# Applying a token norm on the outputs of the projections instead of on their input, and reordering gate products, FFN pairs and attention gates

## The chip, the cores and the metric

The kernel runs on one core of one Trainium2 chip, in one launch. The metric is the device time of that core in microseconds. "PE" is the matrix engine (TensorE), "PEld" its weight loads, DVE the vector engine, ACT the scalar engine, POOL the GpSimd engine and SP the engine that issues the large transfers.

## The reference

Two transformer blocks run one after the other on 256 tokens of width 2048, in fp32. The first has a neighbourhood attention of 16 heads and a convolutional FFN of width 5504. The change touches the FFN's first weights and the whole of the second block, whose core is:

```
def hybrid_layer(x, ...):
    h = rms_norm_2(x, norm_g)
    proj = jnp.einsum('bsd,dn->bsn', h, w_in)
    (q_a, k_a, v_a, o_a, i_a, f_a, z_a, c_q, c_kv, k_r, z_b, g_a, g_b) = jnp.split(proj, offsets, axis=-1)
    qk_a = jax.nn.silu(causal_depthwise_conv(jnp.concatenate([q_a, k_a], axis=-1), conv_w))
    ...
    h_a = mlstm_chunkwise(q_a, k_a, v_a, i_a + bias, f_a + bias)
    h_a = rms_norm_2(h_a, mlstm_norm_g)
    y_a = jnp.einsum('bsc,cd->bsd', jax.nn.sigmoid(o_a) * h_a * jax.nn.silu(z_a), w_a)
    q_b = jnp.einsum('bsr,rn->bsn', rms_norm_2(c_q, q_lat_g), w_uq)
    kv_b = jnp.einsum('bsr,rn->bsn', rms_norm_2(c_kv, kv_lat_g), w_ukv)
    ...
    o_b = causal_attention(q_b, k_b, v_b)
    y_b = jnp.einsum('bsc,cd->bsd', o_b * jax.nn.silu(z_b), w_b)
    y = jax.nn.sigmoid(g_a) * y_a + jax.nn.sigmoid(g_b) * y_b
    return x + jnp.einsum('bsd,de->bse', y, w_out)
```

`rms_norm_2(x, g)` is x times g times one factor per token, r = 1/sqrt(mean of x squared over the 2048 channels + 1e-6). Since r belongs to the token and the product with w_in runs over the channels, (x g r) w_in and ((x g) w_in) r are the same number. The mLSTM has 8 heads (q and k of 128, v of 256), the attention 16 heads (q and k of 128 + 64 with rotation by cos and sin of position times frequency, v of 128).

## The kernel before

*Products.* Everything is kept with channels on the 128 partitions and the 256 tokens along the free axis. An fp32 product is made of three reduced ones: a weight is split into a high half `whi` (a CAST on ACT) and a low half `wlo` (a subtraction on DVE), and so are the activations (`h` = [hH | hL], `hf`, `ya`, `ob`, `latkv`, ...). `GemmW` (L476) makes the products of one output chunk: per input chunk of 128 channels one matmul with `whi` over 512 columns (high and low half of the activation at once) and one with `wlo` over 256 columns. The two column halves of the PSUM bank are added when the bank is read (`fold`, L1056: a COPY on ACT, a sum on DVE).

*Units.* The program is a list of units. A unit is a weight load of 1 MB into one of three raw buffers and the matmuls that use it (`Unit`, L179), and it is split in two halves, each a tile of `whi` and one of `wlo` of 128x1024, from rings of 5. `pair_units` (L1070) cuts a product with 2048 input channels for `nj` output chunks (2 or 4; a bank per output chunk) into pairs of chunks, and each pair into two units: input chunks 0 to 7, then 8 to 15, with 32 matmuls each.

*Order.* The order of the instructions on every engine is fixed when the program is built. `run_units` (L389) goes through the units, and for each emits its matmuls; between them it polls a heap of pending steps (`spawn`, `poll`), which are Python generators: each emits a few instructions on DVE, ACT or POOL and says after which estimated delay it goes on (`yield 1.0`; a bare `yield` is "when the estimate of the last instruction ends"). `Engine` (L136) holds the estimates of cost, and `need` (L230) runs the heap until a condition holds, for instance that a ring has a free tile. The weight halves are emitted up to four ahead (`prep_ahead`, L373). So ACT's, DVE's and POOL's queues each hold weight work and bank work in one order, and an instruction that waits holds up all that stand behind it.

*The stages around the change, with their start in the trace.* In the FFN (`ffn_units`, L1239; from 750 us) a pair of gate chunks is followed by the pair of up chunks; its input chunks `hf` are made by DVE, 16 of them, and a matmul's `need` asks for the chunk it reads. The second block begins with `c_begin` (L1308; near 1490 us). Its input is `h2` = x times norm_g_2, split in halves. The sum of squares and r come from `stats_end` (L1041) as a row form `r2` (128x256, the same row on each partition). The first group of q, k and o products (g = 0 in `ml_qk`, `ml_o`) reads the `h2` that is not normalised, and multiplies its banks with `r2`. Meanwhile a loop in `c_begin` with `h2_again` (L1363) normalises `h2` in place, chunk by chunk: a sum on DVE (`mct`), a product with `r2` on POOL, a CAST on ACT (`hH`), a subtraction on DVE (`hL`). `counted` tells the loop how far the o products, which were put in turn with the k products for it, have read. All later products (`ml_v`, `misc`, `ml_z`, `latent`, `mla_z`, the gates) wait by `h2need` for the new chunks.

`rope_tables` (L1370) is spawned after that loop: two small loads on POOL's queue, an angle, its halves (`angh` by ACT), then some 50 small POOL steps that reduce it, then two ACT steps `rsin`, `rcos`, emitted after `yield 1.0`.

The eight mLSTM heads (`ml_head`, L1578) follow in pairs of heads, `W` being the masked and weighted score, `mv` the value, `ha` the head's output, which is transposed by PE (L265) and becomes `ya`. Then come `gated` units (L1940), four steps `cg` of: a gate product (4 output chunks of g_a), and the product `ya` times w_a for the same chunks, multiplied with the sigmoid (`sga`) when read. Then `latent` (L1663; `latq`, `latkv`, with a norm of their own through `cc`), the attention's heads in pairs: `mla_units` (L1836) are the q and kv products of a pair, `mla_z` (L1730) the four gates `zb` of two pairs, `mla_attn` (L1868) the head, with `bp` the scores after the exponential, `bpt` their transposes, `bv` the values and `ob` the gated output. Then four `gated` steps with g_b and w_b, and the last product.

Of the kernel before, what the change touches and what calls it, by code (L numbers as in the profile page):

```python
# [527 lines left out]
class Model(Kern):  # L528
# [512 lines left out]
    def stats_end(self, width, b, r):  # L1041
# [4 lines left out]
        yield from self.rsqrt(c[:, 0:2], c[:, 12:14], width, c[:, 4:8])  # L1046
        yield
        b = self.bank()
        self.spread(b.t, c[:, 0:2])
# [189 lines left out]
    def ffn_units(self):  # L1239
# [68 lines left out]
    def c_begin(self):  # L1308
# [3 lines left out]
        p = self.L.push("ya")  # L1312
        self.ya = p.tile([128, KD, 512], F32R, name="ya")
# [6 lines left out]
        self.sgring = Ring(self, p, "sga", [128, 256], F32, 5)  # L1320
# [7 lines left out]
        self.soring = Ring(self, p, "so", [128, 256], F32, 5)  # L1328
# [4 lines left out]
        self.fring = Ring(self, p, "fold2", [128, 256], F32, 3)  # L1333
# [12 lines left out]
        r = self.r2 = p.tile([128, 256], F32, name="r2")  # L1346
        self.c_ready = True
        yield from self.stats_end(D, sums, r)
        self.r_ready = True
        for m in range(KD):  # L1350
            while m >= self.early_done:
                yield 0.3
            yield from self.calm()
            t, i = self.cring.get()
            h, l = self.h2H[:, m], self.h2L[:, m]
            self.tt(t, h.bitcast(F32), l.bitcast(F32), ALU.add)
            yield
            self.tt(t, t, r, ALU.mult, e=self.G)
            self.spawn(self.h2_again(m, t, i), max(0.0, self.ct - self.now) + 0.1)
            yield  # L1360
        self.spawn(self.rope_tables(p), 1.0)

    def h2_again(self, m, t, i):  # L1363
        self.A.copy(out=self.h2H[:, m], in_=t)
        yield
        self.V.tensor_sub(out=self.h2L[:, m], in0=t, in1=self.h2H[:, m])
        self.cring.put(i)
        self.h2_ready.add(m)

    def rope_tables(self, p):  # L1370
# [34 lines left out]
        yield 1.0  # L1405
# [22 lines left out]
    def misc(self, out, b):  # L1428
        g8 = slice(0, 8)
        self.A.copy(out=self.krx2[0:64], in_=out[0:64])  # L1430
        a, z, ga, gb, gc = self.gi, self.gz, self.ga, self.gb, self.gc
        self.V.tensor_copy(out=a, in_=out[64:72])
        self.V.tensor_copy(out=z, in_=out[96:104])
# [65 lines left out]
    def h2need(self, k):  # L1499
        self.need(lambda: k in self.h2_ready)  # L1500
# [7 lines left out]
    def ml_qk(self, g, isq):  # L1508
        def evac(j, halves, b):
            h = 2 * g + j  # L1510
            blk = h if isq else 8 + h
            self.need(lambda: self.c_ready and (g or self.r_ready))
# [651 lines left out]
```

## Time and profile before

| | |
|---|---|
| median of 3 runs | 2649.54 us (2644.38 to 2654.28) |
| profiled execution | 2648.81 us |
| its span | 2647.0 us, mean granted clock 0.989 |
| HBM | 511.35 MB read, 196 GB/s over the span |
| DVE, low halves of weights | 822 instructions, 982.5 us, mean 1208 ns |
| ACT, high halves of weights | 822 instructions, 829.6 us, mean 1021 ns |
| chain that ended last | PE 91%, DVE 5%, ACT 2%, POOL 1% |

The profiled execution is one execution of the program; the span runs from its first to its last instruction. In a row of the timeline the numbers are start and busy time in us, then engine, line, operation, output<-inputs, shape and count, and in brackets the idle time ahead of it with what ended it. L151 is the line of the helper that emits every DVE, ACT and POOL instruction, so these are told apart by their tiles. In a window's row there are, per engine, busy us and (instructions), then PE's granted clock as a share of full speed, the busy share of the DMA engines and GB/s.

### The profile page before, as it was taken

Reading aid. Unit: us, or ns where it says so; the run is one execution under the profiler, and the core shown is the slowest. Engines: PE = TensorE matmul, PEld = TensorE weight load, DVE = VectorE, ACT = ScalarE, POOL = GpSimd, SP = SyncE. Lnnn points to the kernel's source line nnn. Section 1 sums busy time; section 2 is a strip of 40 time slices with the busy share of each in tenths; the row PEclk is TensorE's granted clock in tenths of the full one; section 3 lists DMA queues with packets and bytes.
Section 4 is the critical chain, followed back from the end, with each engine's and each line's share of the span. In section 5 each row is a group of like instructions: output and inputs, shape, how many; then the busy total and the mean of one; then the engine's idle time right before and its main releaser. Section 6 shows DMA issues by size and latency. Waiting matters only on the chain.

```text
span 2647.0 us, 40673 instructions
## 1 busy us (share of the span) xinstructions
PE 2563.6 (97%) x16038; PEld 2276.6 (86%) x16038; DVE 1824.0 (69%) x2962; ACT 1430.5 (54%) x2638; POOL 256.7 (10%) x279
## 2 busy tenths in 40 slices
PE   4999999999989999999999998999989999999999
PEld 2799999999968888888888877888878888888888
DVE  7987777677678887877555786567555566766654
ACT  5664444445555555555444556666644467775442
POOL 5421111111110000000000052000000000000000
PEclk8999999999999999999999999999999999999999
DMA  7886776665545666665565544554455533435554
GB/s 268 294 251 227 195 234 211 202 194 194 201 182 211 235 223 223 229 219 207 201 210 195 203 144 152 182 184 163 165 181 207 199 138 129 153 139 199 194 200 155
DMA packets 82543, 522.37 MB, mean 197 GB/s; under 512 B 9232, under 2 KB 15376, under 8 KB 23856
## 3 DMA queue, kind: packets, MB, share of 16 engines
q1 hardware_dynamic: 76656, 501.88, 53.2%
q0 software_dynamic: 5696, 17.90, 4.1%
q8 instruction: 126, 2.06, 0.3%
q14 instruction: 65, 0.53, 0.1%
HBM read 511.35 MB, written 8.39 MB: 196 GB/s over the span
## 4 chain that ended last, share of the span: by engine, by line
PE 91%; DVE 5%; ACT 2%; POOL 1%; issue 1%; DMA 0%; SPq 0%; DVEq 0%; ACTq 0%; POOLq 0%
PE bank L256 89%; DVE wlo L151 2%; PE bank L265 2%; POOL ry L151 1%; ACT whi L151 0%; ACT L149 0%; DVE hL L151 0%; DMA nx<-in_ctxT_dram 0%; DVE mct L151 0%; DVE h L151 0%; POOL racc L151 0%; DVE hf L151 0%; SPq L707 0%; POOL rn L151 0%; DVE cc L151 0%
## 5 line engine op out<-in xcount | busy, mean ns | idle before, releaser
L151 DVE TENSOR_TENSOR wlo<-raw,whi 128x1024 fp32r<-128x1024 f32 (+3 forms) x822 | 982.5, 1208 | 255.8 <-ACT whi L151 252.3
L151 ACT CAST whi<-raw 128x1024 fp32r<-128x1024 f32 (+3 forms) x822 | 829.6, 1021 | 414.0 <-PE bank L256 332.3
L256 PE MATMUL bank<-h,whi 128*128 128x512 f32 (+1 forms) x1696 | 597.5, 397 | 3.5 <-ACT whi L151 3.5
L256 PE MATMUL bank<-hf,whi 128*128 128x512 f32 x1376 | 484.9, 398 | 5.1 <-DVE hf L151 5.1
L256 PE MATMUL bank<-h,wlo 128*128 128x256 f32 x1680 | 473.0, 282 | 0.5 <-DVE wlo L151 0.5
L256 PEld LDWEIGHTS bank<-h,whi 128*128 128x128 f32 x1696 | 319.0, 189 | 78.0 <-ACT whi L151 3.7
L256 PE MATMUL bank<-hf,wlo 128*128 128x256 f32 x1376 | 385.8, 280 | 0.0
L256 PE MATMUL bank<-whi,hH 128*128 128x256 f32 x1280 | 366.6, 286 | 0.0
L256 PE MATMUL bank<-whi,hL 128*128 128x256 f32 x1280 | 362.4, 283 | 2.2 <-DVE hL L151 2.2
L256 PE MATMUL bank<-wlo,hH 128*128 128x256 f32 x1280 | 362.6, 283 | 1.2 <-DVE wlo L151 1.2
L256 PEld LDWEIGHTS bank<-h,wlo 128*128 128x128 f32 x1680 | 319.4, 190 | 1.1 <-DVE wlo L151 1.0
L256 PEld LDWEIGHTS bank<-hf,whi 128*128 128x128 f32 x1376 | 259.0, 188 | 68.8 <-DVE hf L151 7.3
L256 PEld LDWEIGHTS bank<-hf,wlo 128*128 128x128 f32 x1376 | 260.6, 189 | 0.0
L256 PEld LDWEIGHTS bank<-wlo,hH 128*128 128x128 f32 x1280 | 245.3, 192 | 2.4 <-DVE wlo L151 1.8
L256 PEld LDWEIGHTS bank<-whi,hL 128*128 128x128 f32 x1280 | 245.2, 192 | 2.5 <-DVE hL L151 2.4
L256 PEld LDWEIGHTS bank<-whi,hH 128*128 128x128 f32 x1280 | 245.2, 192 | 0.9
L256 PE MATMUL bank<-hid,whi 128*128 128x512 f32 x688 | 243.1, 399 | 0.0
L256 PE MATMUL bank<-hid,wlo 128*128 128x256 f32 x688 | 193.3, 281 | 0.0
L151 DVE SCALAR_TENSOR_TENSOR acc<-raw,cs,acc 128x512 f32<-128x512 f32 x240 | 186.8, 778 | 6.8
L256 PEld LDWEIGHTS bank<-hid,whi 128*128 128x128 f32 x688 | 129.3, 188 | 32.1
L151 ACT COPY fold<-bank 128x256 f32<-128x256 f32 x118 | 43.8, 372 | 165.4 <-PE bank L256 162.6
L256 PEld LDWEIGHTS bank<-hid,wlo 128*128 128x128 f32 x688 | 130.1, 189 | 0.0
(329 smaller groups left out, 3718.2 us busy)
## 6 DMA issues: line engine op xcount, KB each, us to landing
raw<-in_w_in_dram SPq DMA_DIRECT2D x120, 1024.0 KB, 4.9
raw<-in_w_ada_dram SPq DMA_DIRECT2D x86, 1024.0 KB, 4.9
raw<-in_ffn_w_up_dram SPq DMA_DIRECT2D x86, 1024.0 KB, 4.9
raw<-in_na_w_qkv_dram SPq DMA_DIRECT2D x42, 1024.0 KB, 4.9
raw<-in_ffn_w_down_dram SPq DMA_DIRECT2D x40, 1024.0 KB, 4.8
raw<-in_na_w_o_dram SPq DMA_DIRECT2D x16, 1024.0 KB, 5.3
raw<-in_w_a_dram SPq DMA_DIRECT2D x16, 1024.0 KB, 4.9
raw<-in_w_b_dram SPq DMA_DIRECT2D x16, 1024.0 KB, 4.9
```

Of the source, the lines that this page charges most:

```text
L151: r = f(*a, **kw)
L256: self.T.matmul(out, lhsT, rhs, start=start, stop=stop)
L265: self.T.transpose(out, in_, self.con("id"))
```

## The change

1. The loop in `c_begin`, `h2_again` and `counted` go. `h2` stays as it is, and each product that reads it multiplies its banks with `r2`, by one DVE instruction behind the `fold`: q, k, o of all groups, `ml_z`, `misc` (three small ones), `latent`, `mla_z`, the gates. `ml_v`, whose tokens are on the partitions, uses a column form `r2c` as the scale of its ACT step and the scalar of its DVE step; `stats_end` keeps that column. `r2` moves to a pool that lives to the end.
2. `gated` returns its gate units and its w units apart, and `ahead` orders them gate 0, gate 1, w 0, gate 2, w 1, gate 3, w 2, w 3. The ring of gate tiles grows from 5 to 8 and lives in another pool.
3. The first pair of the FFN is emitted as gate unit 0, up unit 0, gate unit 1, up unit 1.
4. `rope_tables` is spawned right after `r2`, and its sines wait 12.0 in place of 1.0 of estimated time.
5. The attention's z pairs stand one pair ahead: pair 0, then for each g pair g + 1 and the units of head pair g.
6. Rings: `fold2` from 3 to 2, `so` from 5 to 4; `latent` takes its scratch tile from another ring.

```
@@ stats_end @@
-    def stats_end(self, width, b, r):
+    def stats_end(self, width, b, r, rc=None):
...
-        yield from self.rsqrt(c[:, 0:2], c[:, 12:14], width, c[:, 4:8])
+        rc = c[:, 0:2] if rc is None else rc
+        yield from self.rsqrt(rc, c[:, 12:14], width, c[:, 4:8])
...
@@ ffn_units @@
+                if not c:
+                    first = [first[0], b[0], first[1], b[1]] if not gate else b
+                    if gate:
+                        continue
+                    b = first
@@ c_begin @@
+        self.sgring = Ring(self, p, "sga", [128, 256], F32, 8)
...
-        self.soring = Ring(self, p, "so", [128, 256], F32, 5)
+        self.soring = Ring(self, p, "so", [128, 256], F32, 4)
...
-        self.fring = Ring(self, p, "fold2", [128, 256], F32, 3)
+        self.fring = Ring(self, p, "fold2", [128, 256], F32, 2)
...
-        yield from self.stats_end(D, sums, r)
+        yield from self.stats_end(D, sums, r, self.r2c)
         self.r_ready = True
-        for m in range(KD):
-            while m >= self.early_done:
-                yield 0.3
-            yield from self.calm()
-            t, i = self.cring.get()
-            h, l = self.h2H[:, m], self.h2L[:, m]
-            self.tt(t, h.bitcast(F32), l.bitcast(F32), ALU.add)
-            yield
-            self.tt(t, t, r, ALU.mult, e=self.G)
-            self.spawn(self.h2_again(m, t, i), max(0.0, self.ct - self.now) + 0.1)
-            yield
         self.spawn(self.rope_tables(p), 1.0)
-    def h2_again(self, m, t, i):
-        self.A.copy(out=self.h2H[:, m], in_=t)
-        yield
-        self.V.tensor_sub(out=self.h2L[:, m], in0=t, in1=self.h2H[:, m])
-        self.cring.put(i)
-        self.h2_ready.add(m)
@@ rope_tables @@
-        yield 1.0
+        yield 12.0
         for t in (sin, cos):
             self.act(t, t, AF.Sin)
@@ h2need @@
-        self.need(lambda: k in self.h2_ready)
+        self.need(lambda: k in self.x2_ready)
@@ ml_qk @@
-            if g == 0:
-                self.tt(u, u, self.r2, ALU.mult)
-                yield
+            self.tt(u, u, self.r2, ALU.mult)
+            yield
@@ ml_v @@
-                    self.split(v[:, 0, j, 0:256], v[:, 1, j, 0:256], out[:, i * 256:i * 256 + 256])
+                    o, r = out[:, i * 256:i * 256 + 256], self.r2c[:, j:j + 1]
+                    self.act(v[:, 0, j, 0:256], o, AF.Copy, scale=r)
+                    self.stt(v[:, 1, j, 0:256], o, r, v[:, 0, j, 0:256].bitcast(F32), ALU.mult, ALU.subtract)
@@ ml_z, latent, mla_z, gated's evac_g, each behind its fold @@
+            self.tt(t, t, self.r2, ALU.mult)
+            yield
@@ gated @@
-        us = self.pair_units("w_in_2", KD, g0 + cg * 512, self.h2p, evac_g, nj=4)
+        gate = self.pair_units("w_in_2", KD, g0 + cg * 512, self.h2p, evac_g, nj=4)
...
-        return us + self.pair_units(w, KD, cg * 512, xs, evac_w, need, lambda: begin(cg), nj=4)
+        return gate, self.pair_units(w, KD, cg * 512, xs, evac_w, need, lambda: begin(cg), nj=4)
+
+    def ahead(self, jobs):
+
+        us = jobs[0][0][:]
+        for cg in range(4):
+            us += (jobs[cg + 1][0] if cg < 3 else []) + jobs[cg][1]
+        return us
@@ c_units @@
-                o = [o[0], o[2], o[1], o[3]]
-                for i in range(2):
-                    o[2 * i + 1].body = self.counted(o[2 * i + 1].body, i)
...
-        for g in range(4):
-            z = self.mla_z(g)
-            us += z[:2] + self.mla_units(2 * g) + z[2:] + self.mla_units(2 * g + 1)
+        z = [u for g in range(4) for u in self.mla_z(g)]
+        us += z[:2]
+        for g in range(8):
+            us += z[2 * g + 2:2 * g + 4] + self.mla_units(g)
```

How the built order moves is shown at three places. A number behind a name is that of a buffer.

ACT's queue where the sines stand. Before, behind the z gates (`mct`) of the first group of heads:

```order
L151 CAST whi<-raw 128x1024
L151 COPY mct_14991<-bank_15785 128x256
L151 CAST whi<-raw 128x1024 x2
L151 COPY mct_14992<-bank_15786 128x256
L151 ACTIVATE mct_14991<-mct_14991 128x256
L151 ACTIVATE rsin<-rsin 128x64
L151 ACTIVATE rcos<-rcos 128x64
L149 ACT_TABLE_LOAD
L151 ACTIVATE E_14998<-E_14998,acol 128x256
```

ACT's queue now: the high part of the angle, `angh`, right behind the first q copy (`mq`), and the sines behind the o gates (`so`), one weight half ahead of the first v copy (`mv`):

```order
L149 ACT_TABLE_LOAD
L151 ACTIVATE mct_14995<-mct_14995 128x256
L151 CAST mq_14983<-mct_14995 128x256
L151 CAST angh<-ang 128x64
L151 CAST whi<-raw 128x1024
L151 COPY fold_15007<-bank_15063 128x256
```

```order
L151 ACTIVATE so_15000<-so_15000 128x256
L151 ACTIVATE so_15001<-so_15001 128x256
L151 CAST whi<-raw 128x1024 x5
L149 ACT_TABLE_LOAD
L151 ACTIVATE rsin<-rsin 128x64
L151 ACTIVATE rcos<-rcos 128x64
L151 CAST whi<-raw 128x1024
L151 ACTIVATE mv_14989<-bank_15425,r2c 128x256
```

Between these two pieces lie 22 rows. The sines have moved from the z product of the first group to a place behind its o product, and `angh` from behind the first `mv` to ahead of it.

PE's queue at the last pair of mLSTM heads, where `W` meets `mv`, where `ha` is transposed and where the first w_a product reads `ya`. Before:

```order
L256 MATMUL bank_18597<-h_12991,whi 128x512
L256 MATMUL bank_18597<-h_12991,wlo 128x256
L256 MATMUL bank_18698<-mv_14985,W_14999 128x258 x3
L256 MATMUL bank_18702<-mv_14985,W_14999 128x258 x6
L265 MATMUL bank_18725<-cons,ha_15000 128x128 x2
L265 MATMUL bank_18725<-cons,ha_15001 128x128 x2
L265 MATMUL bank_18759<-cons,ha_15000 128x128 x2
L265 MATMUL bank_18759<-cons,ha_15001 128x128 x2
L256 MATMUL bank_18772<-ya,whi 128x512
L256 MATMUL bank_18772<-ya,wlo 128x256
```

Now the same two `W` rows, and the transposes of `ha` further down (the first `ya` row comes 32 rows behind them):

```order
L256 MATMUL bank_18680<-h_12991,whi 128x512
L256 MATMUL bank_18680<-h_12991,wlo 128x256
L256 MATMUL bank_18694<-mv_14990,W_15003 128x258 x3
L256 MATMUL bank_18698<-mv_14990,W_15003 128x258 x6
L256 MATMUL bank_18681<-h_12991,whi 128x512
L256 MATMUL bank_18681<-h_12991,wlo 128x256
```

```order
L256 MATMUL bank_18814<-h_12991,whi 128x512
L256 MATMUL bank_18814<-h_12991,wlo 128x256
L265 MATMUL bank_18867<-cons,ha_15004 128x128 x2
L265 MATMUL bank_18867<-cons,ha_15005 128x128 x2
L256 MATMUL bank_18813<-h_12991,whi 128x512
L256 MATMUL bank_18813<-h_12991,wlo 128x256
```

Between W and the transposes there are now rows of a gate product (`h`), where nothing stood before, and more of it between the transposes and `ya`.

PE's queue at the first attention heads, where keys (`bkt`) and scores (`bp`) are transposed. Before, a product of the next pair follows:

```order
L265 MATMUL bank_21074<-cons,bkt_20096 128x128 x2
L265 MATMUL bank_21075<-cons,bkt_20096 128x128
L265 MATMUL bank_21074<-cons,bkt_20096 128x128 x2
L265 MATMUL bank_21075<-cons,bkt_20096 128x128
L265 MATMUL bank_21082<-cons,bp_20100 128x128 x3
L265 MATMUL bank_21088<-cons,bp_20101 128x128 x3
L256 MATMUL bank_21104<-whi,latkv 128x512
L256 MATMUL bank_21104<-wlo,latkv 128x512
L256 MATMUL bank_21104<-whi,latkv 128x512 x2
```

Now the transposed scores of two heads (`bpt`) are used right behind:

```order
L265 MATMUL bank_21178<-cons,bkt_20097 128x128 x2
L265 MATMUL bank_21179<-cons,bkt_20097 128x128
L265 MATMUL bank_21178<-cons,bkt_20097 128x128 x2
L265 MATMUL bank_21179<-cons,bkt_20097 128x128
L265 MATMUL bank_21186<-cons,bp_20101 128x128 x3
L265 MATMUL bank_21193<-cons,bp_20102 128x128 x3
L256 MATMUL bank_21218<-bpt_20103,bv_20087 128x256 x3
L256 MATMUL bank_21218<-bpt_20103,bv_20087 128x128 x3
L265 MATMUL bank_21225<-cons,bsq_20096 128x128 x2
L265 MATMUL bank_21226<-cons,bx_20100 128x128
L265 MATMUL bank_21225<-cons,bsq_20096 128x128 x2
L265 MATMUL bank_21226<-cons,bx_20100 128x128
```

The first two heads of the attention are no longer separated from their own transposes by the next pair's `latkv` product.

## Rows read from the trace of the kernel before

**Rows 1.** The page, part 1: busy us (share of the span) x instructions
```profile
PE 2563.6 (97%) x16038; PEld 2276.6 (86%) x16038; DVE 1824.0 (69%) x2962; ACT 1430.5 (54%) x2638; POOL 256.7 (10%) x279
```

**Rows 2.** Windows of 50 us: PE, PEld, DVE, ACT, POOL, clock, DMA share, GB/s
```profile
1500.00:1550.00 50.00, 45.86 (x232) 38.61 (x231) 42.85 (x69) 31.38 (x52) 12.31 (x11) 0.93 0.49 169
1550.00:1600.00 50.00, 49.12 (x276) 41.59 (x276) 37.90 (x64) 24.53 (x43) 37.45 (x52) 1.00 0.46 153
1600.00:1650.00 50.00, 43.08 (x216) 35.73 (x215) 33.60 (x73) 36.15 (x64) 5.43 (x15) 0.93 0.36 125
1700.00:1750.00 50.00, 50.00 (x265) 42.48 (x264) 35.61 (x69) 39.91 (x70) 0.00 (x0) 1.00 0.43 148
1900.00:1950.00 50.00, 41.98 (x240) 36.64 (x239) 26.45 (x50) 29.86 (x51) 0.00 (x0) 0.93 0.43 148
1950.00:2000.00 50.00, 50.00 (x291) 44.11 (x290) 28.67 (x34) 24.09 (x33) 1.15 (x2) 1.00 0.57 197
2100.00:2150.00 50.00, 45.98 (x251) 39.24 (x251) 29.27 (x54) 27.45 (x48) 0.00 (x0) 0.97 0.42 143
2350.00:2400.00 50.00, 46.30 (x263) 40.06 (x262) 34.78 (x90) 34.66 (x84) 0.87 (x2) 0.93 0.36 127
```

**Rows 3.** Two fine windows, columns as in rows 2
```profile
1541.00:1547.00 6.00, 5.98 (x14) 4.73 (x15) 6.00 (x9) 3.33 (x6) 4.20 (x4) 0.50 0.70 246
2393.00:2397.00 4.00, 3.52 (x11) 3.04 (x12) 4.00 (x13) 3.88 (x11) 0.00 (x0) 0.52 0.16 68
```

**Rows 4.** Timeline of PE, second gate unit of the FFN
```profile
765.81 0.51 PE L256 MATMUL bank<-hf,whi 128*128 128x512 f32 x1 [1.43 <-DVE hf L151]
767.12 0.50 PE L256 MATMUL bank<-hf,whi 128*128 128x512 f32 x1 [0.69 <-DVE hf L151]
```

**Rows 5.** Timeline of PE, first v product of the second block
```profile
1541.02 1.22 PE L256 MATMUL bank<-whi,h 128*128 128x512 f32 x2 [2.46 <-DVE h L151]
```

**Rows 6.** Groups by form, DVE, 1480 to 2500: busy us, mean ns, idle before
```profile
L151 DVE TENSOR_TENSOR h<-mct,h 128x256 fp32r<-128x256 f32 x16 | 10.4, 649 | 0.0
L151 DVE TENSOR_TENSOR mct<-h 128x256 f32<-128x256 f32 x16 | 9.3, 584 | 0.0
L151 DVE TENSOR_TENSOR y<-y,sga 128x256 f32<-128x256 f32 x16 | 6.8, 424 | 0.5
```

**Rows 7.** Timeline of ACT, the sines
```profile
1603.37 0.26 ACT L151 ACTIVATE rsin<-rsin 128x64 f32<-128x64 f32 x1 [8.99 <-POOL rsin L151]
```

**Rows 8.** Timeline of PE behind the sines
```profile
1644.09 0.50 PE L256 MATMUL bank<-wlo,h 128*128 128x512 f32 x1 [2.94 <-DVE wlo L151]
```

**Rows 9.** Timeline of POOL, first and last steps of the sines' argument
```profile
1569.88 0.37 POOL L151 TENSOR_SCALAR ry<-angh 128x64 f32<-128x64 f32 x1 [5.48 <-ACT angh L151]
...
1602.44 0.90 POOL L151 TENSOR_SCALAR rsin<-rsin 128x64 f32<-128x64 f32 x2
```

**Rows 10.** Timeline of ACT, first copy of q and of v
```profile
1507.44 0.41 ACT L151 CAST mq<-mct 128x256 fp32r<-128x256 f32 x1
...
1562.15 0.37 ACT L151 CAST mv<-bank 128x256 fp32r<-128x256 f32 x1 [1.63 <-PE bank L256]
```

**Rows 11.** Timeline of PE, last mLSTM head
```profile
1916.10 1.25 PE L256 MATMUL bank<-mv,W 128*128 128x258 f32 x9
...
1925.81 1.09 PE L265 MATMUL bank<-cons,ha 128*128 128x128 f32 x4 [8.02 <-DVE ha L151]
```

**Rows 12.** Timeline of PE, behind the latent products
```profile
2141.95 0.43 PE L265 MATMUL bank<-cons,cc 128*128 128x128 f32 x2 [2.45 <-DVE cc L151]
...
2143.94 0.52 PE L256 MATMUL bank<-whi,latkv 128*128 128x512 f32 x1 [1.56 <-ACT latkv L151]
```

**Rows 13.** Timeline of PE, last attention heads and first w_b product
```profile
2388.68 0.38 PE L256 MATMUL bank<-bpt,bv 128*128 128x256 f32 x1 [1.13 <-ACT bpt L151]
...
2390.03 2.61 PE L256 MATMUL bank<-bpt,bv 128*128 128x256 f32 x11 [0.96 <-DVE bpt L151]
...
2393.48 0.79 PE L256 MATMUL bank<-ob,whi 128*128 128x512 f32 x1 [0.85 <-DVE ob L151]
```

More of the change, by code (lines that the diff above doesn't have):

```diff
@@ L1045, in stats_end @@
         self.sums(c[:, 12:14], b)
-        yield from self.rsqrt(c[:, 0:2], c[:, 12:14], width, c[:, 4:8])
+        rc = c[:, 0:2] if rc is None else rc
+        yield from self.rsqrt(rc, c[:, 12:14], width, c[:, 4:8])
         yield
         b = self.bank()
-        self.spread(b.t, c[:, 0:2])
+        self.spread(b.t, rc)
         self.ccring.put(ci)
@@ L1319, in c_begin @@
         self.sskr = p.tile([128, 32], F32, name="sskr")[:, 0:2]
-        self.sgring = Ring(self, p, "sga", [128, 256], F32, 5)
+        r = self.r2 = p.tile([128, 256], F32, name="r2")
+        self.r2c = p.tile([128, 32], F32, name="r2c")[:, 0:2]
         p = self.R.push("ml")
@@ L1429, in misc @@
         g8 = slice(0, 8)
-        self.A.copy(out=self.krx2[0:64], in_=out[0:64])
         a, z, ga, gb, gc = self.gi, self.gz, self.ga, self.gb, self.gc
-        self.V.tensor_copy(out=a, in_=out[64:72])
-        self.V.tensor_copy(out=z, in_=out[96:104])
+        for o, x in ((self.krx2[0:64], slice(0, 64)), (a, slice(64, 72)), (z, slice(96, 104))):
+            self.tt(o, out[x], self.r2[x], ALU.mult)
         b.free()
@@ L1511, in evac @@
             blk = h if isq else 8 + h
-            self.need(lambda: self.c_ready and (g or self.r_ready))
+            self.need(lambda: self.r_ready)
             u, ui = yield from self.fold(halves, b, self.fring)
@@ L1552, in evac @@
             t, i = yield from self.fold(halves, b, self.soring)
-            if not g:
-                self.tt(t, t, self.r2, ALU.mult)
-                yield
+            self.tt(t, t, self.r2, ALU.mult)
+            yield
             self.act(t, t, AF.Sigmoid)
@@ L1566, in evac @@
             t, i = yield from self.fold(halves, b, self.cring)
+            self.tt(t, t, self.r2, ALU.mult)
+            yield
             self.act(t, t, AF.Silu)
@@ L1668, in evac @@
                 st["f"] = self.obF[:, 12:16] if name == "q" else self.obF[:, 8:12]
-                st["a"], st["ai"] = self.tring.get()
+                st["a"], st["ai"] = self.sqring.get()
+                st["a"] = st["a"].rearrange("p a b c -> p (a b c)")
             a, f = st["a"], st["f"][:, j]
             yield from self.fold_to(f, halves, b)
+            self.tt(f, f, self.r2, ALU.mult)
+            yield
             if j == 0:
@@ L1700, in chain @@
                 self.split(d[:, 0, j], d[:, 1, j], f)
-            self.tring.put(st["ai"])
+            self.sqring.put(st["ai"])
             self.lat_ready.add(name)
@@ L1708, in mla_begin @@
         self.R.pop("y")
+        self.sgring = Ring(self, self.L.push("sgb"), "sgb", [128, 256], F32, 8)
         p = self.R.push("obf")
@@ L1732, in evac @@
             t, i = yield from self.fold(halves, b, self.zring)
+            self.tt(t, t, self.r2, ALU.mult)
+            yield
             self.act(t, t, AF.Silu)
@@ L1944, in evac_g @@
             t, i = yield from self.fold(halves, b, self.sgring)
+            self.tt(t, t, self.r2, ALU.mult)
+            yield
             self.act(t, t, AF.Sigmoid)
@@ L2032, in out_units @@
         return us
-    def counted(self, inner, i):
-        def run(k0, nk, hi, lo):
-            yield from inner(k0, nk, hi, lo)
-            self.early_done = 8 * i + k0 + nk
-        return run
     def c_units(self):
@@ L2043, in c_units @@
         self.so = {}
-        self.h2_ready, self.x2_ready, self.x2_left = set(), set(), {}
-        self.early_done = 0
+        self.x2_ready, self.x2_left = set(), {}
         self.c_ready = self.r_ready = False
@@ L2065, in c_units @@
                 us += qk + v + o + z
-        for cg in range(4):
-            us += self.gated(cg, 11344, "w_a_2", lambda k: self.ya[:, k], True, self.wa_begin)
+        us += self.ahead([self.gated(cg, 11344, "w_a_2", lambda k: self.ya[:, k], True, self.wa_begin) for cg in range(4)])
         lat = self.latent(8208, "qlg", "q")
@@ L2070, in c_units @@
         us += lat + self.latent(8720, "kvlg", "kv")
-        for g in range(4):
-            z = self.mla_z(g)
-            us += z[:2] + self.mla_units(2 * g) + z[2:] + self.mla_units(2 * g + 1)
-        for cg in range(4):
-            us += self.gated(cg, 13392, "w_b_2", lambda k: self.ob[:, k], False, self.wb_begin)
+        z = [u for g in range(4) for u in self.mla_z(g)]
+        us += z[:2]
+        for g in range(8):
+            us += z[2 * g + 2:2 * g + 4] + self.mla_units(g)
+        us += self.ahead([self.gated(cg, 13392, "w_b_2", lambda k: self.ob[:, k], False, self.wb_begin) for cg in range(4)])
         return us + self.out_units()
```

5 lines of the change are left out of this document (1 added, 4 removed).

## The prediction

> **What bounds the kernel now.** The page's busy line comes first [rows 1]: PE is busy for 97% of the span, DVE 69%, ACT 54%, POOL 10%. PE is the bound, so an edit that only adds or removes work on DVE, ACT or POOL moves the end only where PE waits for that work. What can be won is the 83.4 us in which PE is idle (2647.0 - 2563.6), and the time in which its clock is halved behind a wait. The first 100 us have a good part of it and are not touched by the diff.
>
> So I cut the trace into stretches of 50 us [rows 2] and read two columns: what PE is short of 50.00, and the granted clock. In the pure gate products (1950) nothing is missing: 291 matmuls in 50 us, 0.172 us each. In every short stretch but one the granted clock is under 1.00 too. Finer windows [rows 3] show one of its two levels, 0.50 (1.2 GHz), just behind a wait: six microseconds from 1541 with PE busy 5.98, so 3.0 us lost that no idle time shows. The row that ended each wait then tells its cause.
>
> **The change part by part.**
>
> 1. *First FFN pairs.* In the second gate unit, which reads input chunks 8 to 15, PE catches up with DVE, which still makes them, and waits 1.43 and 0.69 us [rows 4]. In the new order the first up unit, which needs only chunks 0 to 7, stands ahead of it: 32 matmuls, 32 x 0.172 = 5.5 us more for DVE. Both waits go: **2.1 us**. The wait for the norm's own chain, ahead of the first of them, stays.
>
> 2. *Norm out of the input.* The second block's v product waits for 16 normalised chunks, each of which goes through DVE, POOL, ACT and DVE again; the longest wait is 2.46 us [rows 5]. From 1500 to 1600 PE is short of 4.14 + 0.88 = 5.0 us, and 3.0 us go to the halved clock: **8.0 us**. After the change v needs what the first q and k products already used, so no wait takes the place of this one.
>
>  What it adds: by the new DVE order 107 products with r2 instead of 8, so 99 more (three of them small), each like the one of the gate stage, 424 ns [rows 6]: 42 us of DVE. It removes 16 x 0.649 and 16 x 0.584, 19.7 us, on DVE, and 16 steps each on POOL and ACT. The net 22 us on DVE are costed at nothing. They spread over 1000 us; from 1700 to 1750, in the middle of the mLSTM heads, DVE is busy 35.6 of 50 us with PE at 50.00 [rows 2], and a group of heads (about 94 us of products) gets 12 of them, 5 us. A bank is given back by the sum ahead of its product, so PE gets its banks no later. If that cover were gone, the low half of a weight would be late next; that is the slower rival.
>
> 3. *Sines.* ACT stands 8.99 us for a sine argument that POOL has not finished [rows 7]; behind it in ACT's queue are the high halves of the weights. PE waits for them, and 2.94 us more at 1644 for a low half [rows 8], before ACT has caught up. The stretch from 1600 is short of 6.92 us at clock 0.93; of that 7% (3.5 us) I count half, since the other half lies inside the waits: **8.6 us**. Does the sine find its argument now? POOL needs from 1569.88 to 1603.34 [rows 9], 33.5 us from the first piece to the finished argument. In the new ACT order the high part of the angle stands right behind the first q copy (1507.44 here) and the sines one weight half ahead of the first v copy (1562.15, less the 8.0 us of part 2: 1554) [rows 10]. That is some 44 us for a chain of 33.5; both the delay of 12 and the 16 POOL products that no longer stand ahead make it so.
>
> 4. *Gates one step ahead, first stage.* PE reaches the transposes of the last head too early: its W products end at 1917.35, and ha comes at 1925.81 [rows 11], so that chain takes 8.5 us with nothing beside it. Now the next gate product moves ahead of the first w product. In the new PE order some 90 matmuls (15 us) lie between the last W and its ha, and 32 (5.5 us) from there to the first ya. The 8.02 us of idle time go, and with it half of the 3.5 us of lost clock: **9.7 us**.
>
> 5. *z pairs ahead of the heads.* Where the latent products end, PE waits 2.45 us for the norm and 1.56 us for the latent [rows 12]. The second z pair (64 matmuls, 11 us) now runs there: 40 matmuls (7 us) stand ahead of the norm's transposes and 14 (2.4 us) behind them, and both waits are shorter than that. The stretch from 2100 is short of 4.02 us and 3% of clock, 1.5 us: **5.5 us**.
>
> 6. *Gates one step ahead, last stage.* The last heads run into the first w product with nothing between: 1.13, 0.96 and 0.85 us [rows 13]. The clock of that stretch is 0.93, 3.5 us; PE is busy in 3.52 of 4 us of it [rows 3], so 3.1 count. With a gate product more ahead of it, 46 matmuls (7 us, six of them small) lie between the last transposes and their bpt and 40 from there to the first ob: **6.0 us**.
>
> 7. *New close places.* With two z pairs in front the six z buffers are full earlier, and the new order puts the first two heads' bpt right behind their transposes, as the trace has it for the last two [rows 13]. The cost lies between 0 (the wait runs beside others) and 2.1 us (1.13 + 0.96) with 3.5 us of clock, 5.6. I take **+2.1**, the row with the same neighbours.
>
> 8. *Rings and pools.* Eight gate buffers hold two gate products at once. The fold ring of 2 and the so ring of 4 still hold what one pair, or one o product, needs. DMAs keep number and size, on SP and on POOL; POOL's queue loses 16 steps ahead of the rope loads. Nothing.
>
> Sum: 2.1 + 8.0 + 8.6 + 9.7 + 5.5 + 6.0 = 39.9, less 2.1 is 37.8 us. The profiled execution took 2648.81 us (0.7 under the median of the runs), so the forecast is **2611 us**, 1.4% less.
>
> **The rivals.**
>
> *The sines still come late: 2620 us.* The products that the change puts on DVE have two inputs in SBUF and run beside POOL's chain. DVE's own sums took 649 ns where POOL worked and 424 where it did not [rows 6]: the two hold each other up. If POOL's chain grows from 33.5 past 44 us, ACT is blocked as before and part 3 (8.6) is not won. Against it: DVE was busy 37.90 of 50 us from 1550 [rows 2] while POOL made it in 33.5. Chance 0.12. The Trainium skill, "SBUF — State Buffer", section "Who interferes with whom", says that a DVE instruction with two SBUF inputs and a GpSimd instruction that reads SBUF exclude each other for the whole instruction; the trace's 649 beside 424 ns agrees, and by this rule more DVE products beside the sine chain are the wrong direction.
>
> *The attention heads lose more: 2622 us.* Counting the matmuls between the transposes and bpt at 0.172 us, six of sixteen heads have under 5 us in the new order, two in the old. Four more could each cost the 1.13 us of rows 13 and half of 3.5 us of clock, 2.9: 11.5 us. For it: the same neighbours did wait. Against: only the first has nothing between. Chance 0.10.
>
> *The new products make weights late: 2670 us, slower.* Place: the twenty blocks of four products each (o, z, the attention's z, gates a, gates b). DVE works in order, so a low half behind four products is 1.7 us later; where PE has used up its prepared halves it waits as at 1644 [rows 8], 2.94 us per block, 59 us. It decides once DVE is full over a stretch, as from 1500 with 42.85 of 50. Against it: 35.6 and 2.7 more stay under that. Chance 0.04.
>
> *The waits only change place: 2643 us.* All chains share ACT and DVE, and a step that PE reaches earlier may meet another late one; if each part keeps most of its wait, some 6 us are left of the gain. Against: the new order has matmuls between in every part. Chance 0.06.
>
> **How the numbers follow.** Forecast 0.68, rivals 0.12, 0.10, 0.04, 0.06. Low end: nothing lost in part 7 and the clock of parts 3 and 4 in full (1.8 each) give 2605; the runs lie within 5 us of their median, so 2602. High end: the rivals at 2620 and 2622 with the same scatter, 2627. Outside are the slower case, the moved waits and a tail. A measurement here tells about 0.5%, 13 us. Faster than 2636 are the forecast and the first two rivals, 0.90, less a little for their tails: 0.88; same 0.08; slower 0.04.
>
> **What would show it.** Right: PE at 50.00 and clock 1.00 in the stretches with the v product, the first ya and the first ob; no idle time of ACT ahead of rsin; no PE wait for h, ha or latkv; some wait for bpt at the first attention heads. Wrong: PE waits for wlo grow outside the first 75 us, or ACT waits over 5 us for POOL.

## The result and the profile after

The changed kernel takes **2608.62 us** (median of 4 runs, 2607.12 to 2611.98) beside 2648.78 us before (4 runs in the same series): a ratio of 0.9849, 95% interval 0.9828 to 0.987. The forecast was 2611 us. The profiled execution took 2611.98 us, the longest of the four, with a span of 2610.2 us against 2647.0.

The page's busy line answers to [rows 1]:

```profile
PE 2550.1 (98%) x16038; PEld 2268.7 (87%) x16038; DVE 1844.4 (71%) x3027; ACT 1420.7 (54%) x2617; POOL 241.3 (9%) x263
```

PE's idle time fell from 83.4 us to 60.1 (2610.2 - 2550.1), 23.3 us less, and the same 16038 matmuls are busy for 13.5 us less. Most of that is the clock, whose mean rose from 0.989 to 0.995: PE's busy time at clock 0.50 fell from 42.6 to 20.3 us in the two traces, and half of the difference is 11.2 us. The other 2.3 us are not told apart from the pace of the matmuls (last section). Together, 23.3 and 13.5 are the 36.8 us by which the span fell. DVE's busy time rose by 20.4 us, where the forecast had 22.

The windows of 50 us, columns as in [rows 2], show where. Stretches shift by what was won before them, so the row from 1900 holds the first `ya` and the row from 2350 the first `ob`, as before:

```profile
750.00:800.00 50.00, 46.39 (x245) 39.31 (x246) 45.30 (x71) 29.55 (x50) 8.81 (x9) 0.91 0.51 181
1500.00:1550.00 50.00, 50.00 (x262) 42.93 (x261) 34.92 (x56) 31.25 (x47) 32.66 (x50) 1.00 0.60 209
1550.00:1600.00 50.00, 49.68 (x295) 42.64 (x294) 36.76 (x67) 30.81 (x48) 3.91 (x2) 1.00 0.48 168
1600.00:1650.00 50.00, 50.00 (x268) 42.95 (x267) 40.71 (x75) 35.81 (x64) 0.00 (x0) 1.00 0.50 174
1700.00:1750.00 50.00, 48.17 (x252) 40.76 (x251) 37.23 (x62) 33.51 (x55) 0.00 (x0) 1.00 0.54 190
1750.00:1800.00 50.00, 49.53 (x286) 42.65 (x284) 30.29 (x53) 32.61 (x51) 0.00 (x0) 1.00 0.43 148
1800.00:1850.00 50.00, 48.63 (x254) 41.45 (x255) 38.82 (x66) 32.84 (x55) 0.00 (x0) 1.00 0.53 190
1900.00:1950.00 50.00, 50.00 (x289) 43.63 (x289) 33.70 (x51) 29.38 (x44) 0.62 (x1) 1.00 0.56 195
2100.00:2150.00 50.00, 49.63 (x275) 42.60 (x274) 36.96 (x77) 33.82 (x74) 1.11 (x2) 1.00 0.52 181
2150.00:2200.00 50.00, 48.79 (x284) 42.81 (x283) 31.95 (x82) 38.14 (x102) 2.98 (x4) 1.00 0.32 115
2350.00:2400.00 50.00, 50.00 (x294) 43.41 (x294) 37.31 (x71) 30.54 (x60) 1.69 (x3) 1.00 0.53 202
```

Every stretch of [rows 2] that was short of 50 us is full or lacks under 0.4 us, at clock 1.00. Something new stands from 1700 to 1850, where before PE was at 50.00: 1.83 + 0.47 + 1.37 = 3.67 us of idle time. And from 2150 PE lacks 1.21 us.

What ends PE's waits is grouped in the view of waits (engine, tile, line <- what it waited for: us in total, times, longest):

```profile
PE bank L256 <- DVE wlo L151: 20.4, 21, 3.3
...
PE bank L256 <- DVE hf L151: 2.6, 3, 2.2
PE bank L265 <- DVE cc L151: 2.4, 1, 2.4
...
PE bank L256 <- DVE bk L151: 1.2, 1, 1.2
```

No wait for `h`, `ha` or `ob` is left ([rows 5], [rows 11] and the `ob` row of [rows 13] have no counterpart). The one wait for `cc` is that of the FFN's norm near 750 us; that of [rows 12] is gone. Most of the waits for `wlo` lie in the first 100 us, as before. Outside the first 75 us they are 4.3 us in six waits, beside 4.6 us in six before. Four of them are new, and make up the idle time from 1700 to 1850. The first two, in PE's timeline:

```profile
1703.34 0.50 PE L256 MATMUL bank<-wlo,h 128*128 128x512 f32 x1 [0.97 <-DVE wlo L151]
...
1707.26 0.50 PE L256 MATMUL bank<-wlo,h 128*128 128x512 f32 x1 [0.86 <-DVE wlo L151]
```

The other two stand at 1800.50 and 1804.42, again 0.97 and 0.86 us: the v products of the third and fourth pair of heads.

The sines' rows, which answer to [rows 7] and [rows 9]. POOL, first step of the argument and last of the sine's, then ACT:

```profile
1504.77 0.45 POOL L151 TENSOR_SCALAR ry<-angh 128x64 f32<-128x64 f32 x1 [9.19 <-ACT angh L151]
...
1537.26 0.90 POOL L151 TENSOR_SCALAR rsin<-rsin 128x64 f32<-128x64 f32 x2
```

```profile
1547.88 0.26 ACT L151 ACTIVATE rsin<-rsin 128x64 f32<-128x64 f32 x1
```

The chain takes 33.4 us (1504.77 to 1538.16; 33.5 before), ACT comes to it 9.7 us later, and waits for nothing.

### The profile page after: what moved, and what is told of

It reads as the page before. It is cut to its first block, busy times and chain, and to the rows that moved or that the text cites. A ratio compares the mean times of both kernels' runs of the same rounds, so it can differ in the third digit from the quotient of the medians.

```text
span 2610.2 us, 40676 instructions
## 1 busy us (share of the span) xinstructions
PE 2550.1 (98%) x16038; PEld 2268.7 (87%) x16038; DVE 1844.4 (71%) x3027; ACT 1420.7 (54%) x2617; POOL 241.3 (9%) x263
## 4 chain that ended last, share of the span: by engine, by line
PE 94%; DVE 4%; ACT 1%; issue 1%; DMA 0%; SPq 0%; DVEq 0%; ACTq 0%
PE bank L256 91%; PE bank L265 2%; DVE wlo L151 2%; DVE hL L151 0%; ACT L149 0%; DMA nx<-in_ctxT_dram 0%; ACT whi L151 0%; SPq L707 0%; DVE hf L151 0%; DVE gb L151 0%; DVE mct L151 0%; DVE cc L151 0%; DVE adaC L151 0%; PE bank L608 0%; DVE acc L151 0%
```

## The experiments

Each program was run on the same chip as the kernel before, whose median was 2651.7 to 2652.2 us in these series (2642 to 2658). The changed kernel, run again beside the last three, took 2606.21 us (2603.29 to 2610.80). Medians here differ by some 3 us without a cause in the programs, so terms under that are read from the traces. A difference with a sign is taken to 2608.62; to 2606.21 it would be 2.4 us more.

**The first FFN pair in turn again.**

```
-                if not c:
-                    first = [first[0], b[0], first[1], b[1]] if not gate else b
-                    ...
```

> The changed kernel, but the first FFN pair again as gate, gate, up, up. Theory: the two waits for hf in the second gate unit (1.43 and 0.69 us before) come back, +2.1 us to about 2611 us; nothing else moves. Rival: the interleaving does nothing, since DVE makes the chunks in time anyway: 2608.6 us and no wait for hf beyond the first chunk.

2611.78 us, +3.2. In PE's timeline the two waits are back, to 0.01 us what they were in [rows 4]:

```profile
764.82 0.50 PE L256 MATMUL bank<-hf,whi 128*128 128x512 f32 x1 [1.44 <-DVE hf L151]
...
766.13 0.80 PE L256 MATMUL bank<-hf,whi 128*128 128x512 f32 x1 [0.70 <-DVE hf L151]
```

**Gate products in step with their w products.**

```
-        us = jobs[0][0][:]
+        us = []
         for cg in range(4):
-            us += (jobs[cg + 1][0] if cg < 3 else []) + jobs[cg][1]
+            us += jobs[cg][0] + jobs[cg][1]
```

> The changed kernel, but each gate product again directly ahead of its own w product, in both stages. Theory: PE waits about 8 us for ha again behind the last mLSTM head (9.7 us with the clock) and about 3 us for bpt and ob behind the last attention heads (6.0 us with the clock): 2608.6 + 15.7 = 2624 us. Rival: these waits went because ACT and DVE have fewer steps to do there now, not because of the order: under 2612 us, both waits small.

2622.90 us, +14.3 (15.7 expected). PE's waits from 1850 to 2400 us:

```profile
PE bank L265 <- DVE ha L151: 8.1, 2, 7.0
PE bank L265 <- DVE bp L151: 2.7, 1, 2.7
...
PE bank L256 <- DVE ob L151: 0.9, 1, 0.9
```

The wait for `ha` is that of [rows 11] again, now in two, 1.06 and 7.00 us for 8.02. At the end of the attention PE waits one step earlier than in [rows 13], for `bp`: 2.66 us, then 0.25 for `bpt` and 0.94 for `ob`, 3.9 us in all where [rows 13] has 2.9. The order is what removed both.

**Sines without the delay.**

```
-        yield 12.0
+        yield 1.0
```

> The changed kernel, but with the delay of 1 in place of 12 ahead of the sines; in ACT's order they then stand five weight halves earlier. Theory A, the delay is needed: ACT reaches them near 1535 us, the sine's argument is ready at 1538.2 and the cosine's at 1541.4, so ACT stands 3 to 7 us with weight halves behind it and PE loses some of it: 2611 to 2616 us. Theory B, the early start of the angle alone made the sines harmless: ACT waits there, but PE does not, 2609 us.

2608.84 us: theory B. ACT waits a little, and PE not at all (its waits for low halves are the four of the changed kernel):

```profile
1536.45 0.26 ACT L151 ACTIVATE rsin<-rsin 128x64 f32<-128x64 f32 x1 [0.53 <-POOL rsin L151]
1538.70 0.26 ACT L151 ACTIVATE rcos<-rcos 128x64 f32<-128x64 f32 x1 [1.99 <-POOL rcos L151]
```

**The kernel before with the delay alone.** The same line, the other way round.

> The kernel before with one edit: the delay of 12 ahead of the sines. In ACT's order they stand some ten rows later. Theory A, delay alone would have done: ACT's 8.99 us of idle time go to under 2 and the time falls by about 8.6 us, to 2640 us. Theory B, the early start is what did it: ACT still waits for POOL and the time stays within 3 us of 2648.8.

2643.40 us (10 runs) beside 2652.22: ratio 0.9961, 0.9945 to 0.9977. That is 8.8 us less, for which 8.6 were expected: theory A. POOL's chain starts as late as before (1569.99 us), and ACT still waits for it, but only 0.23 us ahead of the sine and 1.98 ahead of the cosine:

```profile
1606.46 0.26 ACT L151 ACTIVATE rsin<-rsin 128x64 f32<-128x64 f32 x1 [0.23 <-POOL rsin L151]
```

PE's waits from 1600 to 1660 us, in the kernel before and with the delay:

```profile
PE bank L256 <- ACT whi L151: 3.5, 1, 3.5
PE bank L256 <- DVE wlo L151: 3.4, 2, 2.9
```

```profile
PE bank L256 <- DVE wlo L151: 0.6, 1, 0.6
```

So either edit, the early start or the delay, removes this wait alone. The changed kernel has both and needs one. The gain in time rests on the medians: the profiled execution is the longest of the ten (2648.32 us), with 6.0 us less idle time of PE than the kernel before and 5.5 us more of busy time, an amount by which the pace of the matmuls can differ (last section).

**Each z pair directly ahead of its heads.**

```
-        us += z[:2]
         for g in range(8):
-            us += z[2 * g + 2:2 * g + 4] + self.mla_units(g)
+            us += z[2 * g:2 * g + 2] + self.mla_units(g)
```

> The changed kernel, but each z pair of the attention directly ahead of its own pair of heads. Theory: the waits for cc (2.45 us) and latkv (1.56 us) behind the latent products come back with their clock, +4.9 us by the two traces, and the waits for bpt at the first heads (0.74 and 0.64 us) go or move: 2608.6 + 3.5 = 2612 us. Rival: the latent products got faster for another reason (the norm leaves the input): 2608 us or less, no wait for cc near 2125 us.

2616.22 us, +7.6 where 3.5 were expected. The waits came back, the first of them longer than in [rows 12]:

```profile
2112.99 0.43 PE L265 MATMUL bank<-cons,cc 128*128 128x128 f32 x2 [3.59 <-DVE cc L151]
2114.98 0.80 PE L256 MATMUL bank<-whi,latkv 128*128 128x512 f32 x1 [1.56 <-ACT latkv L151]
```

3.59 us for 2.45 at `cc`; at `latkv` it is the 1.56 of before. From PE's transposes of the squares to `cc` the chain is no longer than it was (2109.02 to 2112.99, 4.0 us; before 2137.72 to 2141.95, 4.2). What moved is the place of these transposes in PE's order: eight matmuls of the latent product stood behind them before, and none does now. The change put a product with r2 ahead of each square; that this is what moved them was not tried by itself. With a z pair in between the wait is gone.

**The norm on the input again, the other parts kept.** The loop over 16 chunks, `h2_again` and `counted` are put back, and the products with r2 stand where they stood before:

```
+            self.tt(t, h.bitcast(F32), l.bitcast(F32), ALU.add)
+            yield
+            self.tt(t, t, r, ALU.mult, e=self.G)
...
-            self.tt(t, t, self.r2, ALU.mult)
-            yield
```

> The changed kernel, but with the token norm applied to the input in place as before (the loop, its copies, the angle spawned behind it), the other parts kept, the delay of 12 ahead of the sines too. Theory: PE waits for h at the v product again with the halved clock, +8.0 us; the angle starts some 50 us later again, so the sines are late or not by what 12 alone gives, 0 to +8.6 us; the new waits for low halves at 1702 to 1804 us (4.0 us) go if the products with r2 cause them: 2608.6 + 4 to + 16.6, 2613 to 2625 us. Rival: the in-place norm costs nothing with the rest in place: under 2611 us.

2616.97 us, +8.4. PE's waits from 1500 to 1660 us:

```profile
PE bank L256 <- DVE h L151: 4.9, 5, 2.5
PE bank L256 <- DVE wlo L151: 0.6, 1, 0.6
PE bank L256 <- ACT h L151: 0.6, 1, 0.6
```

The waits for `h` are those of before, [rows 5] among them, and the granted clock is 0.50 again behind them, from 1535 us for 6.8 us. The sines are not late for PE, by the delay alone: ACT waits 0.46 and 3.01 us for POOL, and PE has one wait for a low half, of 0.6 us at 1632 us. From 1690 to 1850 us this program has no wait for a low half. So the wait at the v products comes with the norm on the outputs; the next two runs ask whether it is the work on DVE. By the traces the norm on the input costs less than the 8.4 us: outside the first 100 us PE is idle for 21.6 us here and for 19.6 in the changed kernel, since the four late low halves are gone, and the lost clock is 2.2 us (half of the 4.37 in which PE is busy at clock 0.50), together 4.2 us. The rest lies within what medians differ by.

**The products with r2 doubled, and left out.** One more instruction behind each, or none in its place while the planner's clock goes on as if it were there:

```
+        self.nc.vector.tensor_tensor(out=t, in0=t, in1=t, op=ALU.max)
```

> The changed kernel with one more DVE instruction of the same shape behind each of the 107 products with r2 (it takes the maximum of the tile with itself, so the values stay); the order of everything else is the same. That is 45 us more on DVE. Theory, the products are hidden: 0 to +5 us, up to 2614 us. Rival, they are what makes low halves late: each of twenty blocks costs PE up to 2.94 us, +20 to +59 us, over 2628 us.

> The changed kernel with the products with r2 left out, but for the three small ones, so the second block's norm is missing in all but the values; the order of everything else is the same. Theory, hidden: 2608.6 us within 1.5 us. Rival, the four new waits for low halves at 1702 to 1804 us (3.9 us of idle time) come from them: 2604 to 2605 us, and these waits are gone.

Doubled: 2610.01 us (2605.50 to 2611.49), +1.4. Left out: 2608.34 us, -0.3. From none to two of them, 78 us of DVE's busy time (1806.4 to 1884.8), the time moves by 1.7 us, less than the runs of one program differ. They are hidden, with the order as it is. And the four new waits are there without them; PE's waits from 1690 to 1850 us with the products left out:

```profile
PE bank L256 <- DVE wlo L151: 3.7, 4, 1.0
```

What is late there is read from the changed kernel's queues. DVE, then ACT, just ahead of the first of these waits:

```profile
1701.73 0.43 DVE L151 TENSOR_TENSOR mq<-mct,mq 128x256 fp32r<-128x256 f32 x1 [3.63 <-ACT mq L151]
1702.07 1.22 DVE L151 TENSOR_TENSOR wlo<-raw,whi 128x1024 fp32r<-128x1024 f32 x1
```

```profile
1696.18 1.99 ACT L151 CAST whi<-raw 128x1024 fp32r<-128x1024 f32 x2
...
1699.54 1.28 ACT L149 ACT_TABLE_LOAD   x1
1700.84 0.42 ACT L151 ACTIVATE mct<-mct 128x256 f32<-128x256 f32 x1
1701.29 0.41 ACT L151 CAST mq<-mct 128x256 fp32r<-128x256 f32 x1
```

The high half that belongs to this low half is the first of the two at 1696.18, done at 1697.22. DVE could have taken it once its last instruction ended at 1698.10, but stood idle for 3.63 us: next in its queue was the low half of q, which waits for ACT's table load, SiLU and copy. PE, which needed the weight, waited 0.97 us. The second wait has the same neighbours (another 2.36 us of idle time of DVE), and so have the third and fourth.

That DVE stands there is not new. Its waits for the high half of q from 1690 to 1850 us, in the kernel before and in the changed one:

```profile
DVE mq L151 <- ACT mq L151: 11.5, 4, 3.4
```

```profile
DVE mq L151 <- ACT mq L151: 12.0, 4, 3.6
```

The program with the norm on the input has 11.6 us of them, and neither it nor the kernel before has a wait of PE for a weight there. What differs is when PE comes. With the norm on the input, the low half behind q's ends at 1709.82 us and PE begins the v product at 1712.45; in the changed kernel it ends at 1703.29 and PE needs it at 1702.37. The runs do not tell which step of the new order took this lead.

**The low half of q and k emitted later.**

```
-            self.split(d[0][:, 0], d[0][:, 1], t)
+            self.A.copy(out=d[0][:, 0], in_=t)
+            yield
+            self.V.tensor_sub(out=d[0][:, 1], in0=t, in1=d[0][:, 0])
```

> The changed kernel, but the low half of q and k is emitted when its high half is estimated to be done, not at once, so that on DVE a weight's low half no longer stands behind it. Theory: the four new waits for low halves (4.6 us by the traces) come from DVE standing in order behind the low half of q, which waits for ACT; they go, 2604 us. Rival: ACT as a whole is late there because of its table loads, and another row waits in their place: 2608 to 2609 us.

2607.24 us, within the scatter of the changed kernel beside it. Of the four waits two are left, of 0.3 us each, but another low half is late earlier on:

```profile
1567.65 0.39 PE L256 MATMUL bank<-h,wlo 128*128 128x256 f32 x1 [1.63 <-DVE wlo L151]
```

So these waits hang on the low half of q ahead of the weight's. Of their 3.7 us (not 4.6, as expected) 0.6 are left and 1.6 stand at the other place, which leaves 1.5 us, too little to see in the medians. The theory has the waits right and the time wrong.

**The product of the transposed scores later, and both edits.**

```
         b.free()
-        yield
+        yield 3.0
```

> The changed kernel, but the product of the transposed scores is emitted 3 us of estimated time later, so other matmuls stand between them. Theory: the waits for bpt near 2175 us (0.74 and 0.64 us) go or shrink to under 0.5 us together, 2607 us. Rival: the chain of the heads after it gets longer and PE waits for ob or bk instead: 2608.6 us or more.

> Both edits of the two runs before. Theory: they add up, 2608.6 - 4.6 - 1.5 = 2602.5 us. Rival: under 2 us in all, since the waits change place.

2604.84 us (2602.73 to 2604.88) and 2606.27 us (2603.16 to 2608.01), beside 2606.21 for the changed kernel. In the first PE waits 0.24 us for `bk` and 0.35 for `bpt` where the changed kernel waits 0.65 and 0.56 for `bpt` (rows of the section on the steps below).

The traces say 0.6 us less there, and 1.0 less of the wait for `bk` (1.2 to 0.2 us); the 1.4 us between the medians can't be told from no change. The two edits do not add up to the 6.1 us that were expected of them. No version here is shown to be faster than the changed kernel.

**The changed kernel once more.** No edit.

> The changed kernel once more, beside the three that follow: 2608.6 us within 3 us; four waits for low halves of about 1 us between 1700 and 1810 us and two waits for bpt near 2175 us in its trace.

2606.21 us. Its trace has the four waits for low halves, 3.7 us in all, and those for `bpt`, 0.7 and 0.6 (the expectation of the run with each z pair ahead of its heads had 0.74 and 0.64).

## Why the prediction was right, step by step

The time came out 2.4 us under the forecast, well inside the range, and most parts came out near theirs. Idle time and clock can be held against the forecast apart: of its 39.9 us, 28.9 were idle time of PE and 11.0 clock. Idle time in the stretches of the six parts, and what the medians say:

| part | forecast idle + clock | idle won by the windows | by experiment |
|---|---|---|---|
| 1 first FFN pairs | 2.1 | 2.5 (waits for hf, 5.1 to 2.6) | 3.2 |
| 2 norm out of the input | 5.0 + 3.0 | 4.7 | 8.4; 4.2 by the traces, net of the new waits |
| 3 sines | 6.9 + 1.7 | 6.9 | 8.8 |
| 4, 6 gates ahead | 8.0 + 1.7, 2.9 + 3.1 | 8.0, 3.7 | 14.3 for both |
| 5 z pairs ahead | 4.0 + 1.5 | 3.7 | 7.6, with part 7 |

For the first row, PE's waits for `hf` before were:

```profile
PE bank L256 <- DVE hf L151: 5.1, 6, 2.2
```

The idle time won in these stretches is 29.5 us. Against it stand new waits of 1.2 and 3.7 us and a first 100 us with 1.0 us more of it, which leaves 23.6; the two busy lines say 23.3. The clock gave back 11.2 us, for which the forecast had 11.0; another 2.3 us of busy time went without the clock.

That the sum is this close is in part luck. The late low halves (3.7 us) and the first 100 us (1.0) had no term in it, and they are made up for by the 0.6 us of idle time won on top, by the 0.9 that part 7 cost less, and by the 2.3 us that no part accounts for. The two profiled executions differ by 36.8 us, the medians by 40.2; the forecast of 37.8 lies between.

- *Part 1, right.* Both waits went, and came back by undoing it.
- *Part 2, right in what it wins; one sentence of it failed.* The first v product waits for nothing. That the products on DVE cost nothing holds, shown from both sides (none and double). But "no wait takes the place of this one" is not so: the four late low halves of 3.7 us stand a stage further on. The forecast looked for late weights as a matter of DVE's busy time, with the point of decision at a full DVE. At 37.23 of 50 us DVE was far from full, and stood idle for 3.63 us ahead of the weight. What counted was one instruction that waits for ACT, ahead of the weight in the queue, at a place where PE had no lead left; a standstill of the same kind, of 3.4 us, cost the kernel before nothing.
- *Part 3, right in size, wrong in its "both".* The forecast said that the delay and the missing POOL products together give the room. Its own numbers held (33.4 us for 33.5; a slack of 9.7 us for 10.5), but either is enough (8.8 us from the delay alone in the old kernel; no loss without it in the new one, where the chain starts early). With only one of them ACT does wait, 2.2 to 3.5 us, and PE by 0.6 us at most.
- *Parts 4 and 6, right.* Taken back, they cost 14.3 us of 15.7.
- *Part 5, right in the waits, short in what it covers.* Both waits are gone but for 0.33 us at `latkv`. Without the z pair in between the one for `cc` is longer in the changed kernel than it was before (3.59 us for 2.45), so this part also hides 1.1 us for which the forecast had no term; that they come from part 2 is not shown.
- *Part 7, right in place, high by 0.9 us.* The waits at the first heads, which answer to [rows 13], are shorter than the 2.1 us taken:

```profile
2175.10 0.38 PE L256 MATMUL bank<-bpt,bv 128*128 128x256 f32 x1 [0.65 <-ACT bpt L151]
2176.04 0.79 PE L256 MATMUL bank<-bpt,bv 128*128 128x256 f32 x5 [0.56 <-DVE bpt L151]
```

- *The rivals.* Sines late: no, since the chain did not grow. Heads that lose more: no; of the six heads with under 5 us of matmuls in between, only the first shows waits for `bpt` in the view of waits (one of each kind). Weights late through DVE's load: not by that mechanism. Waits that change place: beside the 29.5 us of idle time won there are 4.9 us of new waits.
- *Its signs.* Those of being right came, but for the 0.33 us at `latkv`. Of those of being wrong, waits for `wlo` outside the first 75 us did not grow in sum (4.6 to 4.3 us), because the 3.4 us behind the sines went while the four new ones came; a sum over the whole span did not show the new place.
- *A slip in the range.* 5 us under 2605 is 2600 and not 2602; nothing rests on it.

## What to carry to other kernels

Where one engine is at 97%, sum its idle time by stretch and add the clock lost behind each wait: a wait of 1 to 8 us cost up to 3.0 us more here, 11 us in all. A chain that PE runs into is best covered by independent products put between its start and its use, and work moved to an engine with idle time was free here even when doubled. Look then at what stands in order ahead of the weights on each engine: an instruction that waits for another engine holds them up although its own engine is idle, and no busy share tells that. It costs time where PE comes for the weight before it is done.

## What the runs showed that was not expected

*Matmuls have more than one pace at clock 1.00.* In the FFN's last product, which no edit here touches, PE is busy without a gap, and the same 150 us (1300 to 1450) hold 851 matmuls in one execution and 867 in another, with DMA and clock alike. The changed kernel, and the one with the products left out:

```profile
1300.00:1450.00 150.00, 150.00 (x851) 130.13 (x850) 80.56 (x100) 64.33 (x80) 3.21 (x6) 1.00 0.61 210
```

```profile
1300.00:1450.00 150.00, 150.00 (x867) 132.25 (x867) 82.34 (x102) 65.44 (x81) 3.22 (x6) 1.00 0.61 212
```

The whole product takes 243.26 us in the one and 238.67 in the other. Both values occurred on one chip within one series, and no wait goes with it. Two executions of the changed kernel itself differ in another stretch, 568 and 579 matmuls from 2400 to 2500. What sets it stays open; 4.6 us for one product is as much as one of the smaller terms, so single spans were not compared for those.

*Of two steps on DVE and POOL, the later one stretches.* In the changed kernel 14 of the 50 steps of the sine chain take over 1 us, and each of the 14 starts within a `wlo` subtraction on DVE; none of the other 36 takes that long, and the seven of them that start 0.12 to 0.41 us ahead of a `wlo` keep 0.37 to 0.59 us. Two of the same kind:

```profile
1512.25 1.31 POOL L151 TENSOR_TENSOR ry<-ry,rn 128x64 f32<-128x64 f32 x1
...
1515.96 0.32 POOL L151 TENSOR_TENSOR ry<-ry,rn 128x64 f32<-128x64 f32 x1
```

From 1512.16 to 1514.71 DVE makes two low halves (1.21 and 1.23 us), and around 1516 it waits. The Trainium skill, "SBUF — State Buffer", section "Who interferes with whom", says that a DVE instruction with two inputs in SBUF and a GpSimd instruction that reads SBUF exclude each other; the trace agrees. POOL bears it here, and the low halves themselves stay between 1.21 and 1.35 us. In the kernel before it is also DVE that bears it, where its sum starts behind a POOL product:

```profile
1541.38 0.85 POOL L151 TENSOR_TENSOR mct<-mct,r 128x256 f32<-128x256 f32 x1 [0.70 <-DVE mct L151]
```

```profile
1541.23 0.41 DVE L151 TENSOR_TENSOR h<-mct,h 128x256 fp32r<-128x256 f32 x1
1541.56 0.95 DVE L151 TENSOR_TENSOR mct<-h 128x256 f32<-128x256 f32 x1
```

The 649 and 584 ns of [rows 6] are thus means of sums of 0.41 and of 0.95 us. In the changed kernel it is the weights' low halves, not the products with r2 of 0.42 us, that stretch POOL's chain: it takes 32.5 us with these products left out, 33.4 with them and 33.0 with two of each.

*The clock fell without a wait.* From 2271 to 2274.8 us PE was busy throughout, with short products of the heads, and then had 3.4 us at half clock, again busy throughout:

```profile
2271.00:2274.80 3.80, 3.80 (x25) 3.11 (x23) 0.97 (x4) 3.75 (x7) 0.00 (x0) 1.00 0.57 207
2274.80:2278.20 3.40, 3.40 (x12) 3.18 (x12) 2.28 (x13) 1.91 (x10) 0.00 (x0) 0.50 0.00 0
```

It cost some 1.7 us (half of 3.4). PE's last wait ahead of it is that for `bk` at 2236 us, and no run here tells its cause. The kernel before has one such fall (2181.8 us, 3.4 us long, PE busy throughout), and of the other programs all but the one with the product of the transposed scores later have one to three among the attention heads with no wait of PE in the 10 us ahead, most of them at other places.
